# Gate matrices from one-hot rows: three bf16 pieces with four tokens innermost, in place of float32

## The chip, the core and the metric

The kernel runs on one NeuronCore of one Trainium2 chip. The metric is device time in microseconds (us). Five engines work side by side and meet at semaphores: TensorE (PE in the rows; PEld is its weight load), VectorE (DVE), ScalarE (ACT), GpSimd (POOL) and SyncE (SP), which issues most DMAs.

## The reference, cut to what matters

The layer is a token mixer followed by a product-key expert mixer (PEER). For every token and each of 8 heads, the mixer scores 128 × 128 experts as the sum of two key scores, keeps the best 16, and takes a softmax over them as gates:

```python
top_s, top_pos = lax.top_k(cand, PEER_TOPK)
idx = jnp.take_along_axis(cand_idx, top_pos, axis=-1)      # i1 * 128 + i2
gate = jax.nn.softmax(top_s, axis=-1)
act = jax.nn.gelu(jnp.einsum("td,thkd->thk", xb, expert_down[idx]))
return jnp.einsum("thk,thkd->td", gate * act, expert_up[idx])
```

There are 512 tokens, width 1024, and 128 picks (8 heads × 16) per token.

## The kernel before, in words

The first 128 tokens gather their experts' rows by indirect DMA. The other 384 (`TD`) do it densely: for all 128 × 128 experts the kernel computes GELU(x · down) on TensorE, multiplies by a gate matrix that is zero for experts that were not picked, and multiplies by `up` on TensorE.

The gate matrix of one token is 128 × 128, indexed by i2 and i1. It is made by a matrix product over the token's 128 picks, which lie on the partitions: one operand holds in row p the one-hot row of i2 times the gate of pick p, the other the one-hot row of i1. This stretch is called the gate stage here. It runs in 96 steps of four tokens (12 groups of 32 tokens, 8 steps each). In every step:

- the two operands `ob` and `oa` are made. In 67 of the 96 steps VectorE makes both: four TENSOR_SCALARs (line 850, one per token, compare with i2 and multiply by the gate) and one TENSOR_TENSOR over the four tokens (line 852, compare with i1). In the other 29 (`ng % 10 in A_ACT`) VectorE makes only the one-hot rows of i2 (line 841), and ScalarE makes the rows of i1 with the gate in them (lines 845 and 846);
- TensorE multiplies them into a PSUM bank `g_ps` (line 857, four float32 matmuls, which the trace shows as eight, two passes each), and ScalarE copies the bank to `stg` (line 860);
- `take` puts some products of another kind between: tiles of x · down (`s_ps`, lines 126 to 128) that are needed later. Their weights are split in a high and a low part, `w_hi` on ScalarE (line 612) and `w_lo` on GpSimd (line 613);
- in 28 of the steps a part of the top-16 search of the first 128 tokens is done on VectorE (`picks`: lines 671 to 721).

After every eighth step `stg` goes to DRAM by SyncE, and a small part to SBUF on GpSimd (line 866). The order on an engine comes from a scheduler that follows the code and its data; TensorE's is tied by `issue_after`. `ob` and `oa` have four buffers each. Behind the gate stage comes the longest stretch, in which TensorE multiplies by `up` (line 941) and makes the other tiles of x · down.

Of the kernel before, what the change touches and what calls it, by code (L numbers as in the profile page):

```python
# [18 lines left out]
P = 128  # L19
# [10 lines left out]
NK = 128  # L30
# [3 lines left out]
TD = NDT * P  # L34
# [38 lines left out]
def hymba_peer_block(ctx, tc, consts, x, nmix, w_in, w_ba, conv_w, a_log, dt_bias, dn_w, w_pool, pool_scale,  # L73
                     w_out, nffn, w_q, sub_k, downT, down, up, nfin, out):
    nc = tc.nc
# [8 lines left out]
    iota = cst[:, C_IO:C_IO + P]  # L84
# [64 lines left out]
    with ExitStack() as fx:  # L149
# [77 lines left out]
        with tc.tile_pool(name="prep", bufs=1) as pr:  # L227
# [59 lines left out]
            for h in range(DNH):  # L287
                for qk, dst in ((0, qT), (1, kT)):
# [3 lines left out]
                    for tb in range(NTB):  # L292
                        o = (tb * DNH + h) * 2 + qk
                        nc.tensor.matmul(ssq[:, o:o + 1], sq[:, tsl(tb)], ones[:, 0:1],
                                         start=(h == 0 and qk == 0 and tb == 0),
                                         stop=(h == 3 and qk == 1 and tb == 3))
            for h in range(DNH):
# [3 lines left out]
                for tb in range(NTB):  # L301
                    nc.tensor.transpose(pv[:, tsl(tb)], vt[:, tsl(tb)], ident)
                nc.vector.tensor_tensor(vb[:, :, h, :], v4(pv), beta[:, :, h:h + 1].broadcast_to([P, NTB, P]),
                                        op=ALU.mult)
# [9 lines left out]
                                           op0=ALU.mult, op1=ALU.mult)  # L314
# [3 lines left out]
            for tb in range(NTB):  # L318
# [3 lines left out]
                for h in range(DNH):  # L322
                    nc.tensor.matmul(gr[:, tsl(h)], gt[:, tb, h:h + 1].broadcast_to([P, P]), umat,
                                     start=(h == 0), stop=(h == 3))
                dt = pr.tile(H4, F32, name="dt")
                for h in range(DNH):
                    o = tb * 4 + h
                    nc.vector.scalar_tensor_tensor(dt[:, h], gr[:, tsl(h)], gcs[:, 0, o:o + 1], m0,
                                                   op0=ALU.subtract, op1=ALU.min)
# [5 lines left out]
                for lhs, dst in ((kT, d["at"]), (qT, d["aq"])):  # L335
# [3 lines left out]
                    for h in range(DNH):  # L339
                        nc.vector.scalar_tensor_tensor(dst[:, h], kk[:, tsl(h)], rqk[:, tb, h, 1:2], dt[:, h],  # L340
                                                       op0=ALU.mult, op1=ALU.mult)
                nc.vector.tensor_mul(qT[:, :, ts], qT[:, :, ts], egr)
                fr = p_dl.tile([P, 512], F32, name="fr", tag="dl")
                for h in range(DNH):
                    nc.tensor.matmul(fr[:, tsl(h)], fco[:, tb, h:h + 1].broadcast_to([P, P]), ident,
                                     start=(h == 0), stop=(h == 3))
# [26 lines left out]
        with ExitStack() as f2:  # L373
# [110 lines left out]
            for tb in range(NTB):  # L484
# [5 lines left out]
                for h in range(DNH):  # L490
                    nc.tensor.matmul(vps[:, tsl(h)], d["tt"][:, h], vb[:, tb, h], start=(h == 0),
                                     stop=(tb == 0 and h == 3))
# [24 lines left out]
                for h in range(DNH):  # L517
                    nc.tensor.matmul(ops[:, tsl(h)], d["aq"][:, h], vn[:, h], start=(tb == 0 and h == 0),
                                     stop=(h == 3))
# [65 lines left out]
    pp = ctx.enter_context(tc.tile_pool(name="pp", bufs=1))  # L585
# [3 lines left out]
    sc0 = pp.tile([P, NG, PH, 2, NK], F32, name="sc0")  # L589
    eidx = [pp.tile([P, NSLOT], I32, name=f"eidx{b}") for b in range(NG)]  # L590
    gat = [pp.tile([P, PH, K], F32, name=f"gat{b}") for b in range(NG)]
    i1t = pp.tile([P, TD], F32, name="i1t")
    n1t = pp.tile([P, TD], F32, name="n1t")
    i2t = pp.tile([P, TD], F32, name="i2t")
    gtt = pp.tile([P, TD], F32, name="gtt")
    ngt = pp.tile([P, TD], F32, name="ngt")

    gp = ctx.enter_context(tc.tile_pool(name="gp", bufs=2))
    up_p = ctx.enter_context(tc.tile_pool(name="up_p", bufs=2))
# [134 lines left out]
    with ExitStack() as fy:  # L734
        tk = fy.enter_context(tc.tile_pool(name="tk", bufs=2))
        p_pj = fy.enter_context(tc.tile_pool(name="p_pj2", bufs=2, space=PSUM))
        p_sc = fy.enter_context(tc.tile_pool(name="p_sc", bufs=4, space=PSUM))
        skt = tk.tile([P, 16, NK], F32, name="skt", bufs=1)
        nc.scalar.dma_start(out=skt, in_=sub_k)
        SA = [P, NDT, PH, K]  # L740
        i1a = tk.tile(SA, F32, name="i1a", bufs=1)
        i2a = tk.tile(SA, F32, name="i2a", bufs=1)
        tsa = tk.tile(SA, F32, name="tsa", bufs=1)

        def query(h, eng):
            qh = tk.tile([P, 2, T], F32, name="qh")
            w = [load_pair(w_q[2 * h + p], eng) for p in range(2)]
            ps = [p_pj.tile([P, 512], F32, name="q_ps") for p in range(2)]
            parts = [slice(0, T)] if h else [slice(0, T // 2), slice(T // 2, T)]
            for ts in parts:  # L750
                for p in range(2):
                    for c in range(DC):
                        mm3(ps[p][:, ts], (w[p][0][:, c, :], w[p][1][:, c, :]), (xn_hi[:, c, ts], xn_lo[:, c, ts]),
                            c == 0, c == DC - 1)
            for p in range(2):
                cp = nc.scalar.copy(qh[:, p], ps[p])
            behind[:] = [None, cp.ins]
            sc = tk.tile([P, NDT, 2, NK], F32, name="sc")
            ps = [p_sc.tile([P, 512], F32, name="sc_ps") for _ in range(NTB)]
            for p in range(2):  # L760
                for tb in range(NTB):
                    nc.tensor.matmul(ps[tb][:, p * NK:(p + 1) * NK], qh[:, p, tb * P:(tb + 1) * P],  # L762
                                     skt[:, 2 * h + p, :], start=(p == 0), stop=(p == 1))
            for tb in range(NTB):
                nc.scalar.copy(sc0[:, tb, h] if tb < NG else sc[:, tb - NG],
                               ps[tb][:, :2 * NK].rearrange("p (a k) -> p a k", a=2))
            return sc

        sc = query(0, nc.vector)
        for h in range(PH):  # L770
            sc_next = query(h + 1, nc.gpsimd) if h + 1 < PH else None
            for _ in topk(tk, sc, NDT, tsa[:, :, h, :], i1a[:, :, h, :], i2a[:, :, h, :]):
                pass
            sc = sc_next
            if sc is not None:
                make_ahead(h + 1)
        make_ahead(S_QUERY + S_WAIT)
        ex = tk.tile(SA, F32, name="ex", bufs=1)
        softmax(tk, ex.rearrange("p b h k -> p (b h) k"), tsa.rearrange("p b h k -> p (b h) k"), s_act[0])


        steps = ahead_steps()
        taken = 0
        pe_last = s_last[0]

        def take(goal):
            nonlocal taken, pe_last
            while taken < goal:
                with tc.issue_after(pe_last.ins):
                    next(steps, None)  # L790
                pe_last = s_last[0]
                taken += 1

        for src, dst in ((i1a, i1t), (i2a, i2t), (ex, gtt)):
            if src is ex:
                take(DC)
            ps = p_pj.tile([P, 512], F32, name="q_ps")
            with tc.issue_after(pe_last.ins):
                for b in range(NDT):
                    pe_last = nc.tensor.transpose(ps[:, b * P:(b + 1) * P], src[:, b].rearrange("p h k -> p (h k)"),  # L800
                                                  ident)
            nc.vector.tensor_copy(dst, ps[:, :TD])
            if dst is not i2t:
                nc.scalar.activation(n1t if dst is i1t else ngt, ps[:, :TD], AF.Copy, scale=-1.0)

    hp.append(ctx.enter_context(tc.tile_pool(name="hp2", bufs=RUN + 1 - RA)))

    with ExitStack() as fy:
# [17 lines left out]
        gs = fy.enter_context(tc.tile_pool(name="gs", bufs=3))  # L826
# [5 lines left out]
        for tg in range(NTG):  # L832
            stg = gs.tile([P, NK, TG], F32, name="stg", bufs=1)
            for q in range(TG // 4):
                oa = gs.tile([P, 4, P], F32, name="oa", bufs=4)
                ob = gs.tile([P, 4, P], F32, name="ob", bufs=4)
                ps = p_g.tile([P, 512], F32, name="g_ps")
                t0 = tg * TG + q * 4
                q4 = [P, 4, P]
                if ng % 10 in A_ACT:  # L840
                    one = nc.vector.tensor_tensor(ob, iota[:, None, :].broadcast_to(q4),  # L841
                                            i2t[:, t0:t0 + 4, None].broadcast_to(q4), op=ALU.is_equal)
                    for u in range(4):
                        t = t0 + u
                        nc.scalar.activation(oa[:, u], iota, AF.Abs, bias=n1t[:, t:t + 1])
                        nc.scalar.activation(oa[:, u], oa[:, u], AF.Relu, scale=ngt[:, t:t + 1], bias=gtt[:, t:t + 1])
                else:
                    for u in range(4):
                        t = t0 + u
                        nc.vector.tensor_scalar(ob[:, u], iota, i2t[:, t:t + 1], gtt[:, t:t + 1], op0=ALU.is_equal,  # L850
                                                op1=ALU.mult)
                    one = nc.vector.tensor_tensor(oa, iota[:, None, :].broadcast_to(q4),  # L852
                                            i1t[:, t0:t0 + 4, None].broadcast_to(q4), op=ALU.is_equal)
                ng += 1
                with tc.issue_after(pe_last.ins):
                    for u in range(4):
                        pe_last = nc.tensor.matmul(ps[:, u * P:(u + 1) * P], ob[:, u], oa[:, u], start=(u == 0),
                                                   stop=(u == 3))
                take(S_FIRST + ng * (n_steps - S_FIRST) // (TD // 4))
                nc.scalar.copy(stg[:, :, q * 4:q * 4 + 4], ps.rearrange("p (t i) -> p i t", i=NK))  # L860
                if ng * n_picks // (TD // 4) > picked:
                    with tc.issue_after(one.ins):
                        next(picks)
                    picked += 1
            sv = stg.rearrange("p i t -> p (i t)")
            nc.gpsimd.tensor_copy(gsb0[:, tg, :], sv[:, :GN * TG])
            nc.sync.dma_start(out=gmat[tg, :, GN * TG:], in_=sv[:, GN * TG:])
# [180 lines left out]
```

## Time and profile before

| | us |
|---|---|
| median of 3 runs | 1597.91 (1595.98 to 1601.22) |
| the profiled execution | 1597.25 |
| its span, first to last instruction | 1595.5 |
| TensorE busy | 1543.3 (97%) |
| TensorE weight loads busy | 1391.5 (87%) |
| VectorE busy | 1291.3 (81%) |
| ScalarE busy | 692.1 (43%) |
| GpSimd busy | 556.9 (35%) |

Busy time is that in which an engine had an instruction in work. Matmuls are pipelined and their ends are modelled, so a busy TensorE need not be at its limit: start-to-start times tell more. The shares are means over stages with different limits, so the gate stage has to be read by itself.

### The profile page before, as it was taken

How to read it: one execution, taken by the hardware profiler on the slowest of the kernel's cores; microseconds unless marked ns; L12 is line 12 of the kernel's file. 1: busy time of each engine (PE TensorE's matmuls, PEld its weight loads, DVE VectorE, ACT ScalarE, POOL GpSimd, SP SyncE). 2: the span in 40 equal slices, each digit the busy share in tenths (PEclk: the TensorE clock that was granted, in tenths of full speed). 3: DMA queues.
4: the chain of work that ended last, by engine and by line, in shares of the span. 5: the costliest groups of instructions: out<-in, count | busy, mean ns of one | idle time of the engine just before them, and what ended most of it. 6: DMA issues, size and time to landing. Idle time of an engine off the chain costs nothing.

```text
span 1595.5 us, 23368 instructions
## 1 busy us (share of the span) xinstructions
PE 1543.3 (97%) x8417; PEld 1391.5 (87%) x8417; DVE 1291.3 (81%) x2652; ACT 692.1 (43%) x1175; POOL 556.9 (35%) x362
## 2 busy tenths in 40 slices
PE   6999999999999899899999999999999999999996
PEld 5889798888899899889888888889989888888885
DVE  5577666699999999996887777778888787888885
ACT  5545343333338687673333333333333333333333
POOL 1000000144464333224454445444444444444331
PEclk9999999999999999999999999999999999999998
DMA  6221221422344455459999999999999999899971
GB/s 210 80 67 55 65 83 41 172 89 85 93 128 149 175 194 220 153 207 387 364 337 327 339 315 317 329 329 334 311 332 311 335 319 334 309 326 340 321 265 61
DMA packets 142388, 367.32 MB, mean 230 GB/s; under 512 B 11232, under 2 KB 65520, under 8 KB 140608
## 3 DMA queue, kind: packets, MB, share of 16 engines
q1 hardware_dynamic: 104416, 228.09, 41.4%
q0 software_dynamic: 37712, 136.69, 23.9%
q8 instruction: 66, 1.08, 0.3%
q10 hardware_dynamic: 144, 1.05, 0.2%
q14 instruction: 50, 0.41, 0.1%
HBM read 331.58 MB, written 34.21 MB: 229 GB/s over the span
## 4 chain that ended last, share of the span: by engine, by line
PE 80%; DVE 17%; ACT 1%; DMA 1%; issue 1%; POOL 1%; SPq 0%; ACTq 0%; DVEq 0%; POOLq 0%
PE acc L941 33%; PE s_ps L126 9%; PE s_ps L128 9%; PE s_ps L127 9%; DVE ob L850 7%; PE pj L127 3%; PE pj L126 3%; PE pj L128 3%; DVE oa L852 3%; PE q_ps L127 2%; PE q_ps L128 2%; PE q_ps L126 2%; PE ups L432 1%; PE p L441 1%; DVE ob L841 1%; PE sc_ps L762 1%
## 5 line engine op out<-in xcount | busy, mean ns | idle before, releaser
L126 PE MATMUL s_ps<-xn_hi,w_hi 128*128 128x384 f32 x1024 | 356.8, 348 | 0.0
L128 PE MATMUL s_ps<-xn_hi,w_lo 128*128 128x384 f32 x1024 | 346.4, 338 | 2.5 <-DVE w_lo L613 1.9
L127 PE MATMUL s_ps<-xn_lo,w_hi 128*128 128x384 f32 x1024 | 345.7, 338 | 0.0
L612 ACT ACTIVATE w_hi<-w_raw 128x1024 fp32r<-128x1024 f32 x144 | 152.9, 1062 | 331.7 <-PE s_ps L127 260.4
L916 POOL DMA_INDIRECT row<-in_down_dram,eidx x128 | 190.0, 1485 | 224.8 <-DVE row L918 194.4
L925 POOL DMA_INDIRECT row<-in_up_dram,eidx x128 | 187.0, 1461 | 222.8 <-DVE xr L927 201.0
L613 POOL TENSOR_TENSOR w_lo<-w_raw,w_hi 128x1024 fp32r<-128x1024 f32 x60 | 153.8, 2564 | 291.1 <-ACT w_hi L612 257.2
L941 PE MATMUL acc<-u_hi,whi 128*128 128x512 f32 x768 | 238.6, 391 | 0.6 <-ACT whi L120 0.6
L941 PE MATMUL acc<-u_lo,whi 128*128 128x512 f32 x768 | 237.6, 389 | 0.0
L941 PE MATMUL acc<-u_hi,wlo 128*128 128x512 f32 x768 | 237.5, 389 | 0.0
L120 ACT ACTIVATE whi<-w 128x384 fp32r<-128x384 f32 x128 | 67.2, 525 | 307.5 <-issue 277.2
L128 PEld LDWEIGHTS s_ps<-xn_hi,w_lo 128*128 128x128 f32 x1024 | 192.9, 188 | 3.5 <-DVE w_lo L613 2.3
L127 PEld LDWEIGHTS s_ps<-xn_lo,w_hi 128*128 128x128 f32 x1024 | 193.2, 189 | 3.2
L126 PEld LDWEIGHTS s_ps<-xn_hi,w_hi 128*128 128x128 f32 x1024 | 193.2, 189 | 3.2
L121 DVE TENSOR_TENSOR wlo<-w,whi 128x384 fp32r<-128x384 f32 x128 | 71.2, 556 | 133.8 <-ACT whi L120 133.6
L927 DVE SCALAR_TENSOR_TENSOR xr<-row,dots,xr 128x1024 f32<-128x1024 f32 x128 | 164.2, 1282 | 9.6 <-DMA row<-in_up_dram,eidx 7.7
L941 PEld LDWEIGHTS acc<-u_lo,whi 128*128 128x128 f32 x768 | 144.3, 188 | 31.3 <-DVE u_lo L121 0.3
L941 PEld LDWEIGHTS acc<-u_hi,wlo 128*128 128x128 f32 x768 | 144.2, 188 | 29.9
L918 DVE SCALAR_TENSOR_TENSOR row<-row,xg 128x1024 f32<-128x1024 f32 x128 | 152.1, 1220 | 15.0 <-DMA row<-in_down_dram,eidx 11.4
L941 PEld LDWEIGHTS acc<-u_hi,whi 128*128 128x128 f32 x768 | 143.0, 188 | 24.4 <-ACT whi L120 0.8
L121 DVE TENSOR_TENSOR u_lo<-u_raw,u_hi 128x1024 fp32r<-128x1024 f32 x128 | 156.0, 1219 | 4.1 <-ACT u_hi L120 4.1
L120 ACT ACTIVATE u_hi<-u_raw 128x1024 fp32r<-128x1024 f32 x128 | 134.3, 1049 | 5.5 <-DMA u_raw<-in_up_dram 2.8
(298 smaller groups left out, 2448.8 us busy)
## 6 DMA issues: line engine op xcount, KB each, us to landing
u_raw<-in_up_dram SPq DMA_DIRECT2D x128, 512.0 KB, 6.2
w_raw<-in_downT_dram SPq DMA_DIRECT2D x128, 512.0 KB, 5.7
gmat<-stg SPq DMA_DIRECT2D x12, 1984.0 KB, 8.4
gsb<-gmat SPq DMA_DIRECT2D x31, 768.0 KB, 7.3
w_raw<-in_w_in_dram SPq DMA_DIRECT2D x20, 512.0 KB, 3.6
w_raw<-in_w_q_dram SPq DMA_DIRECT2D x16, 512.0 KB, 3.6
hfar<-h_far SPq DMA_DIRECT2D x26, 192.0 KB, 2.0
h_act<-hfar SPq DMA_DIRECT2D x26, 192.0 KB, 5.9
```

Of the source, the lines that this page charges most:

```text
L120: nc.scalar.activation(hi, src, AF.Copy)
L121: nc.vector.tensor_sub(lo, src, hi.bitcast(F32))
L126: nc.tensor.matmul(ps, ahi, bhi, start=first, stop=False)
L127: nc.tensor.matmul(ps, ahi, blo, start=False, stop=False)
L128: return nc.tensor.matmul(ps, alo, bhi, start=False, stop=last)
L612: nc.scalar.activation(hi, raw, AF.Copy)
L613: eng.tensor_sub(lo, raw, hi.bitcast(F32))
L916: nc.gpsimd.indirect_dma_start(out=r, out_offset=None, in_=down, in_offset=bass.IndirectOffsetOnAxis(ap=eidx[b][:, s:s + 1], axis=0))
L918: nc.vector.scalar_tensor_tensor(r, r, 1.0, xg, op0=ALU.mult, op1=ALU.mult, accum_out=dots[:, s:s + 1])
L925: nc.gpsimd.indirect_dma_start(out=r, out_offset=None, in_=up, in_offset=bass.IndirectOffsetOnAxis(ap=eidx[b][:, s:s + 1], axis=0))
L927: nc.vector.scalar_tensor_tensor(xr[b], r, dots[:, s:s + 1], xr[b], op0=ALU.mult, op1=ALU.add)
L941: nc.tensor.matmul(acc[b][n], l[:, bs], r[:, n * 512:(n + 1) * 512], start=(i == 0 and l is whi and r is uhi), stop=(i == NK - 1 and l is ...
```

## The change

The gate is no longer a factor in float32. Ahead of the stage it is split into three bf16 pieces whose sum is the float32 gate (`gpc`), by three casts and two subtractions on VectorE. The one-hot rows and the pieces are bf16, and the tiles have the four tokens of a step innermost. Each step now makes the one-hot rows of i2 (`oh2`), multiplies them by the three pieces in one TENSOR_TENSOR (`ob`, 3 × 128 × 4 elements), and makes the rows of i1 (`oa`); in the 29 steps with ScalarE's help ScalarE makes only `oa`, now without the gate. TensorE adds three bf16 products per token.

```diff
-    i1t = pp.tile([P, TD], F32, name="i1t")
+    i1t = pp.tile([P, TD], BF16, name="i1t")
     n1t = pp.tile([P, TD], F32, name="n1t")
-    i2t = pp.tile([P, TD], F32, name="i2t")
+    i2t = pp.tile([P, TD], BF16, name="i2t")
     gtt = pp.tile([P, TD], F32, name="gtt")
-    ngt = pp.tile([P, TD], F32, name="ngt")
+    gpc = pp.tile([P, 3, TD], BF16, name="gpc")
+    iota4 = pp.tile([P, NK, 4], BF16, name="iota4")
+    nc.vector.tensor_copy(iota4, iota[:, :, None].broadcast_to([P, NK, 4]))
...
+        for j in range(3):
+            nc.vector.tensor_copy(gpc[:, j], gtt)
+            if j < 2:
+                nc.vector.tensor_sub(gtt, gtt, gpc[:, j])
...
-                oa = gs.tile([P, 4, P], F32, name="oa", bufs=4)
-                ob = gs.tile([P, 4, P], F32, name="ob", bufs=4)
+                oa = gs.tile([P, NK, 4], BF16, name="oa", bufs=4)
+                oh2 = gs.tile([P, NK, 4], BF16, name="oh2", bufs=2)
+                ob = gs.tile([P, 3, NK, 4], BF16, name="ob", bufs=4)
...
+                nc.vector.tensor_tensor(oh2, iota4, i2t[:, None, t4].broadcast_to(q4), op=ALU.is_equal)
+                one = nc.vector.tensor_tensor(ob, oh2[:, None].broadcast_to(p4), gpc[:, :, None, t4].broadcast_to(p4),
+                                              op=ALU.mult)
                 if ng % 10 in A_ACT:
-                    one = nc.vector.tensor_tensor(ob, iota[:, None, :].broadcast_to(q4),
-                                            i2t[:, t0:t0 + 4, None].broadcast_to(q4), op=ALU.is_equal)
                     for u in range(4):
-                        t = t0 + u
-                        nc.scalar.activation(oa[:, u], iota, AF.Abs, bias=n1t[:, t:t + 1])
-                        nc.scalar.activation(oa[:, u], oa[:, u], AF.Relu, scale=ngt[:, t:t + 1], bias=gtt[:, t:t + 1])
+                        ab = gs.tile([P, P], F32, name="ab", bufs=2)
+                        nc.scalar.activation(ab, iota, AF.Abs, bias=n1t[:, t0 + u:t0 + u + 1])
+                        nc.scalar.activation(oa[:, :, u], ab, AF.Relu, scale=-1.0, bias=1.0)
                 else:
-                    for u in range(4):
-                        t = t0 + u
-                        nc.vector.tensor_scalar(ob[:, u], iota, i2t[:, t:t + 1], gtt[:, t:t + 1], op0=ALU.is_equal,
-                                                op1=ALU.mult)
-                    one = nc.vector.tensor_tensor(oa, iota[:, None, :].broadcast_to(q4),
-                                            i1t[:, t0:t0 + 4, None].broadcast_to(q4), op=ALU.is_equal)
+                    one = nc.vector.tensor_tensor(oa, iota4, i1t[:, None, t4].broadcast_to(q4), op=ALU.is_equal)
                 ng += 1
                 with tc.issue_after(pe_last.ins):
                     for u in range(4):
-                        pe_last = nc.tensor.matmul(ps[:, u * P:(u + 1) * P], ob[:, u], oa[:, u], start=(u == 0),
-                                                   stop=(u == 3))
+                        for j in range(3):
+                            pe_last = nc.tensor.matmul(ps[:, u * P:(u + 1) * P], ob[:, j, :, u], oa[:, :, u],
+                                                       start=(u == 0 and j == 0), stop=(u == 3 and j == 2))
```

VectorE's order near the start of the gate stage, before. The rows L671 to L676 are the top-16 search; `ob` and `oa` are the operands of a step.

```order
L841 TENSOR_TENSOR ob<-cst,i2t 128x512
L850 TENSOR_SCALAR ob<-cst,i2t,gtt 128x128 x4
L852 TENSOR_TENSOR oa<-cst,i1t 128x512
L850 TENSOR_SCALAR ob<-cst,i2t,gtt 128x128 x4
L852 TENSOR_TENSOR oa<-cst,i1t 128x512
L671 MAX val<-sc_2702 128x8
L672 MAX_INDEX idx<-val,sc_2702 128x8
L674 MATCH_REPLACE rep<-val,sc_2702 128x128
```

The same place in VectorE's order of the changed kernel (the search's lines are L673 to L678 there, `oh_…` are the buffers of `oh2`):

```order
L673 MAX val<-sc_2702 128x8
L850 TENSOR_TENSOR oh_5007<-iota_2710,i2t 128x512
L674 MAX_INDEX idx<-val,sc_2702 128x8
L676 MATCH_REPLACE rep<-val,sc_2702 128x128
L851 TENSOR_TENSOR ob<-oh_5007,gpc 128x1536
L677 MAX val<-rep 128x8
L850 TENSOR_TENSOR oh_5047<-iota_2710,i2t 128x512
L678 MAX_INDEX idx<-val,rep 128x8
L851 TENSOR_TENSOR ob<-oh_5047,gpc 128x1536
L859 TENSOR_TENSOR oa<-iota_2710,i1t 128x512
L850 TENSOR_TENSOR oh_5073<-iota_2710,i2t 128x512
L859 TENSOR_TENSOR oa<-iota_2710,i1t 128x512
```

Every gate instruction is now a TENSOR_TENSOR with two operands in SBUF, and the scheduler puts some other instruction between an `oh2` and the `ob` that reads it: in all 96 steps the two are not neighbours. The search's instructions stand more thinly among them.

TensorE's order around one step of the gate stage, before:

```order
L127 MATMUL s_ps<-xn_lo,w_hi 128x384
L128 MATMUL s_ps<-xn_hi,w_lo 128x384
L857 MATMUL g_ps<-oa,ob 128x128 x4
L126 MATMUL s_ps<-xn_hi,w_hi 128x384
L127 MATMUL s_ps<-xn_lo,w_hi 128x384
```

And in the changed kernel (the first and the last of the twelve gate products):

```order
L128 MATMUL s_ps<-xn_hi,w_lo 128x384
L864 LDWEIGHTS ob
L864 MATMUL g_ps<-oa,ob 128x128
L864 LDWEIGHTS ob
L864 MATMUL g_ps<-oa,ob 128x128
...
L864 LDWEIGHTS ob
L864 MATMUL g_ps<-oa,ob 128x128
L126 MATMUL s_ps<-xn_hi,w_hi 128x384
```

The gate products stand at the same place among the tiles of x · down, twelve pairs of weight load and matmul in place of four float32 matmuls. GpSimd's order is the same in both.

## Rows read from the trace of the kernel before

**Rows 1.** Page, part 1: busy us, share of span, instructions.
```profile
PE 1543.3 (97%) x8417; PEld 1391.5 (87%) x8417; DVE 1291.3 (81%) x2652; ACT 692.1 (43%) x1175; POOL 556.9 (35%) x362
```

**Rows 2.** Windows: the gate stage, and what follows it.
```profile
core 0: us, PE busy (x) PEld busy (x) DVE busy (x) ACT busy (x) POOL busy (x), PEclk, DMA share, GB/s
482.60:711.30 228.70, 211.24 (x1442) 206.19 (x1441) 226.42 (x622) 170.70 (x388) 75.69 (x39) 0.99 0.51 184
711.30:1595.50 884.20, 869.23 (x4270) 777.40 (x4270) 700.11 (x900) 315.14 (x440) 387.31 (x264) 0.99 0.89 315
```

**Rows 3.** Chain of waits inside the gate stage, shares by line (cut by the view).
```profile
by line: DVE ob L850 47.8%; DVE oa L852 17.6%; DVE ob L841 7.6%; DVE rep L674 2.7%; DVE idx L672 2.5%; DVE idx L676 2.2%; DVE oh L714 2.1%; DVE i L721 2.1%; DVE oh L717 2.1%; DVE val L675 1.7%; DVE val L671 1.5%; DVE idf L686 1.3%; DVE ta L
```

**Rows 4.** Groups of instructions in the gate stage: count | busy us, mean ns.
```profile
L850 DVE TENSOR_SCALAR ob<-cst,i2t,gtt 128x128 f32<-128x128 f32 x268 | 117.4, 489 | 0.0
...
L126 PE MATMUL s_ps<-xn_hi,w_hi 128*128 128x384 f32 x225 | 84.7, 377 | 0.0
...
L841 DVE TENSOR_TENSOR ob<-cst,i2t 128x512 f32<-128x512 f32 x29 | 19.7, 679 | 0.0
```

**Rows 5.** Single lines: count, duration ns min/median/max, first and last start.
```profile
L850 DVE TENSOR_SCALAR ob<-cst,i2t,gtt x268: 320/336/2433, 483.7 to 705.0; 128x128 f32<-128x128 f32 x134
L852 DVE TENSOR_TENSOR oa<-cst,i1t x67: 662/679/691, 483.1 to 705.3; 128x512 f32<-128x512 f32 x67
L717 DVE TENSOR_TENSOR oh<-oh,idf x4: 685/690/2870, 543.3 to 708.6; 128x1024 bf16<-128x1024 bf16 x4
L717 DVE TENSOR_TENSOR oh<-oh,idf x8: 959/1996/3205, 331.5 to 470.8; 128x1536 bf16<-128x1536 bf16 x8
L714 DVE TENSOR_TENSOR oh<-fij,cst x8: 1757/1758/1761, 329.8 to 469.0; 128x1536 bf16<-128x1536 f32 x8
L704 DVE TENSOR_SCALAR ta<-pos x4: 167/172/2391, 540.1 to 705.9; 128x32 uint32<-128x32 uint32 x4
L686 DVE CAST idf<-idx x4: 184/313/2399, 523.8 to 690.9; 128x64 bf16<-128x64 uint32 x4
L613 POOL TENSOR_TENSOR w_lo<-w_raw,w_hi x27: 2362/2481/3127, 483.1 to 696.5; 128x1024 fp32r<-128x1024 f32 x27
```

**Rows 6.** VectorE in order of time, gate stage: start us, duration us.
```profile
494.90 3.18 DVE L850 TENSOR_SCALAR ob<-cst,i2t,gtt 128x128 f32<-128x128 f32 x4
498.01 0.68 DVE L852 TENSOR_TENSOR oa<-cst,i1t 128x512 f32<-128x512 f32 x1
498.61 1.10 DVE L850 TENSOR_SCALAR ob<-cst,i2t,gtt 128x128 f32<-128x128 f32 x4
499.63 0.68 DVE L852 TENSOR_TENSOR oa<-cst,i1t 128x512 f32<-128x512 f32 x1
```

**Rows 7.** GpSimd (first row) and VectorE in order of time around 602 us.
```profile
602.16 3.13 POOL L613 TENSOR_TENSOR w_lo<-w_raw,w_hi 128x1024 fp32r<-128x1024 f32 x1 [2.56 <-ACT w_hi L612]
...
601.77 0.68 DVE L852 TENSOR_TENSOR oa<-cst,i1t 128x512 f32<-128x512 f32 x1
602.37 0.68 DVE L841 TENSOR_TENSOR ob<-cst,i2t 128x512 f32<-128x512 f32 x1
602.97 0.29 DVE L671 MAX8 val<-sc 128x8 f32<-128x128 f32 x1
...
603.83 1.55 DVE L850 TENSOR_SCALAR ob<-cst,i2t,gtt 128x128 f32<-128x128 f32 x1
```

**Rows 8.** TensorE in order of time, one gate step and its neighbours.
```profile
563.38 1.05 PE L857 MATMUL g_ps<-oa,ob 128*128 128x128 f32 x8
564.19 0.42 PE L126 MATMUL s_ps<-xn_hi,w_hi 128*128 128x384 f32 x1
564.45 0.34 PE L127 MATMUL s_ps<-xn_lo,w_hi 128*128 128x384 f32 x1
...
565.33 1.05 PE L857 MATMUL g_ps<-oa,ob 128*128 128x128 f32 x8
```

More of the change, by code (lines that the diff above doesn't have):

```diff
@@ L802, in hymba_peer_block @@
             nc.vector.tensor_copy(dst, ps[:, :TD])
-            if dst is not i2t:
-                nc.scalar.activation(n1t if dst is i1t else ngt, ps[:, :TD], AF.Copy, scale=-1.0)
+            if dst is i1t:
+                nc.scalar.activation(n1t, ps[:, :TD], AF.Copy, scale=-1.0)
+        for j in range(3):
+            nc.vector.tensor_copy(gpc[:, j], gtt)
+            if j < 2:
+                nc.vector.tensor_sub(gtt, gtt, gpc[:, j])
     hp.append(ctx.enter_context(tc.tile_pool(name="hp2", bufs=RUN + 1 - RA)))
@@ L834, in hymba_peer_block @@
             for q in range(TG // 4):
-                oa = gs.tile([P, 4, P], F32, name="oa", bufs=4)
-                ob = gs.tile([P, 4, P], F32, name="ob", bufs=4)
+                oa = gs.tile([P, NK, 4], BF16, name="oa", bufs=4)
+                oh2 = gs.tile([P, NK, 4], BF16, name="oh2", bufs=2)
+                ob = gs.tile([P, 3, NK, 4], BF16, name="ob", bufs=4)
                 ps = p_g.tile([P, 512], F32, name="g_ps")
                 t0 = tg * TG + q * 4
-                q4 = [P, 4, P]
+                t4 = slice(t0, t0 + 4)
+                q4 = [P, NK, 4]
+                p4 = [P, 3, NK, 4]
+                nc.vector.tensor_tensor(oh2, iota4, i2t[:, None, t4].broadcast_to(q4), op=ALU.is_equal)
+                one = nc.vector.tensor_tensor(ob, oh2[:, None].broadcast_to(p4), gpc[:, :, None, t4].broadcast_to(p4),
+                                              op=ALU.mult)
                 if ng % 10 in A_ACT:
-                    one = nc.vector.tensor_tensor(ob, iota[:, None, :].broadcast_to(q4),
-                                            i2t[:, t0:t0 + 4, None].broadcast_to(q4), op=ALU.is_equal)
                     for u in range(4):
-                        t = t0 + u
-                        nc.scalar.activation(oa[:, u], iota, AF.Abs, bias=n1t[:, t:t + 1])
-                        nc.scalar.activation(oa[:, u], oa[:, u], AF.Relu, scale=ngt[:, t:t + 1], bias=gtt[:, t:t + 1])
-                else:
-                    for u in range(4):
-                        t = t0 + u
-                        nc.vector.tensor_scalar(ob[:, u], iota, i2t[:, t:t + 1], gtt[:, t:t + 1], op0=ALU.is_equal,
-                                                op1=ALU.mult)
-                    one = nc.vector.tensor_tensor(oa, iota[:, None, :].broadcast_to(q4),
-                                            i1t[:, t0:t0 + 4, None].broadcast_to(q4), op=ALU.is_equal)
+                        ab = gs.tile([P, P], F32, name="ab", bufs=2)
+                        nc.scalar.activation(ab, iota, AF.Abs, bias=n1t[:, t0 + u:t0 + u + 1])
+                        nc.scalar.activation(oa[:, :, u], ab, AF.Relu, scale=-1.0, bias=1.0)
+                else:
+                    one = nc.vector.tensor_tensor(oa, iota4, i1t[:, None, t4].broadcast_to(q4), op=ALU.is_equal)
                 ng += 1
```

## The prediction

> **What bounds the kernel now.** I read the page first. TensorE is busy 97% of the span and VectorE 81% [rows 1], which suggests a kernel bound by TensorE all through. The change, however, touches one stretch only, so the windows come next: from 482.6 to 711.3 us, 228.7 us, VectorE is busy 226.4 us and TensorE 211.2 us; behind it, for 884 us, TensorE is busy 869 us and VectorE 700 us [rows 2]. The reader is to see that the engine which is nearly full changes at these borders. The chain of waits in the stretch decides which of the two it is: its shares are VectorE's, line by line; L850, L852 and L841, the three instructions that make one-hot rows, have 73% between them, and the rest is the search [rows 3]. So the gate stage is as long as VectorE's queue. A saving on TensorE buys nothing there, and an instruction added on VectorE is paid in full.
>
> What is in VectorE's 228.7 us? The order of time gives the cost from start to start: the four TENSOR_SCALARs of a step 1.02 us (498.61 to 499.63), the TENSOR_TENSOR 0.60 us (498.01 to 498.61) [rows 6]. The same four took 3.11 us at 494.90. Those 2.09 us more are a hold. GpSimd's subtraction `w_lo` (27 in the stage, 2.36 us at least) and VectorE keep each other out: the longest TENSOR_SCALAR took 2433 ns where the median is 336 [rows 5]. The holds add up to 268 × (489 − 336) ns = 41.0 us on L850 [rows 4, 5], and one each of 2.2, 2.2 and 2.1 us on L717, L704 and L686 (maximum less median) [rows 5]: 47.5 us, 1.76 us per `w_lo`.
>
> **The change part by part.**
>
> *A bf16 TENSOR_TENSOR.* The stage has one already: L717 multiplies bf16 by bf16, one operand a short row that is read again and again, as here. Unheld it takes 685 ns for 1024 elements and 959 for 1536, so 274 ns per 512; on float32 input L714 takes 1758 ns for 1536 [rows 5]. So it runs at twice the rate, with some 137 ns fixed. 512 elements then take 411 ns. Successive instructions overlap by 0.08 us (679 ns long, 600 from start to start) [rows 5, 6], so `oh2` or `oa` costs 0.33 us of queue and `ob` (1536) 0.88 us.
>
> *Steps in which VectorE makes both operands, 67.* Before 1.02 + 0.60 = 1.62 us, now 0.33 + 0.88 + 0.33 = 1.54: 67 × (−0.08) = −5.4 us.
>
> *Steps in which ScalarE makes `oa`, 29* [rows 4]. Before, VectorE had one instruction of 0.60 us, because the gate went into ScalarE's half. Now the gate is on VectorE's side in every step: 0.33 + 0.88 = 1.21. That is 29 × 0.61 = +17.7 us, the largest term. It lies on VectorE's queue, which nothing covers. ScalarE, busy 170.7 of 228.7 us [rows 2], had room, and its small saving is worth nothing.
>
> *The split of the gate.* Two subtractions of 384 columns, at most 0.60 × 384/512 = 0.45 us each, and three casts, between the cast row L686 (0.2 to 0.3 us for 64 columns) and 0.45: +1.9 us on the same queue, ahead of the first `ob`. The copy that makes `iota4` stands before the search, is no dearer than the 0.60 us of L852, and gets 0 here and 0.6 at the upper end.
>
> *The holds.* An `oh2` has to be done before its `ob` starts, but the order always has another instruction between the two, so I add no gap there. What changes is how GpSimd meets VectorE. At 602.16 a `w_lo` came while one TENSOR_TENSOR ran, and a second followed directly; `w_lo` took 3.13 us, 0.77 more than its least, so it was let in only as the second one ended. Then four search instructions ran beside it, and the next TENSOR_SCALAR took 1.55 us, a hold of 1.21 [rows 7]. That the search's instructions run beside `w_lo` is why the mean hold is 1.76 and not 2.09. In the new order gate instructions stand between the search's, so after one or two of them a gate instruction is in front and waits. Bounds: at the top 27 × 2.09 = 56 us, +9; at the bottom no hold at all, −47.5. I take 2.0 us each, 54 us, +6.5, because the row that is like the new instructions (L717, two bf16 operands in SBUF) was held for 2.2 us.
>
> [...]
>
> *TensorE.* From one gate block to the next is 1.95 us with six `s_ps` passes at 0.176 us (564.45 to 565.33 is five starts), so a block costs 1.95 − 1.06 = 0.89 us, eight passes of 0.112 [rows 8]. 96 × 0.89 + 674 × 0.176 = 85 + 119 = 204 us of 228.7 (674 is about three lines of 225 [rows 4]). No bf16 product of 128 columns is in the trace. From below it costs a third of a 384-column pass, 0.059 us; from above what a float32 pass of 128 columns costs, 0.112. Twelve make 0.70 to 1.34 us, 96 times that 68 to 129, and the stage's TensorE work 187 to 248 us. I take the middle, 0.085, since the columns speak for the first and a weight load for every product for the second: 217 us. VectorE's new stage is longer than even the upper end, so TensorE adds 0 to the sum; this cover is thin there, and the first rival prices it.
>
> [...]
>
> *Elsewhere* nothing is added or removed. The 884 us behind the stage start when VectorE's queue and the last gate matrices are done, so they shift with it.
>
> *Sum.* The profiled execution took 1597.25 us (1.75 more than its span), 0.7 less than the median of the runs. −5.4 + 17.7 + 1.9 + 6.5 = +20.7: 1618 us. The forecast's own range goes from holds that stay as they are, with the casts at their least (1610), to holds at their top with 0.6 us for `iota4` and a few us of TensorE's lag (1626).
>
> **The rivals.**
>
> *TensorE becomes the bound.* It decides from 0.113 us per product, where 1152 × 0.113 + 119 = 249 us is VectorE's new length. In favour: twelve weight loads per step, where a load takes part in a price of 0.112 now; and a TensorE that waits more may be granted less than the 0.99 of full clock [rows 2]; against: half the bytes per element. At 0.13 the stage is 269 us, +40, 1637.
>
> *The doubled rate does not come.* The repeated row of L717 is 16 bf16 long, here it is four. At the float32 rates (0.60 and 1758 − 80 = 1.68 us) a step costs 2.88 instead of 1.62 and 2.28 instead of 0.60: 84 + 49 = +133, with the split and the holds 1739 us. [...]
>
> *Faster: the holds end.* One mechanism: TENSOR_SCALARs waited for `w_lo`, TENSOR_TENSORs of the gate don't, as the 67 of L852 never did [rows 5]. Then 41.0 us of L850 go, and the rest of the sum, +14.2, stays: 1597.25 + 14.2 − 41.0 = 1570 us. It comes out faster as soon as more than 14.2 us of holds go in all, that is, below 1.2 us per `w_lo`. A partial form is likelier than the full one: GpSimd, kept waiting by back-to-back TENSOR_TENSORs, gets in beside the search and holds little.
>
> *No change.* The holds fall by some 14 us and just pay for the rest: 1597.
>
> **How the numbers follow.** Forecast 0.60 (1618). TensorE as the bound 0.14. Single rate 0.05. Faster 0.11. No change 0.10. Under 0.3%, some 5 us, a difference cannot be told from none here. Slower is 0.60 + 0.14 + 0.05 = 0.79, same 0.10, faster 0.11. The range reaches down to 1596, which leaves out the faster cases and a little of no change (about 0.13), and up to 1645, which takes in TensorE at 0.13 and leaves out the single rate (with the worst of TensorE, 0.07).
>
> **What would show it.** In the changed profile the gate stage should be about 249 us, with VectorE busy nearly all of it and named in the chain; `oh2` and `oa` about 0.41 us, `ob` about 0.96 us, and a few of either near 2.4 us or above; the sum of these excesses near 54 us; `w_lo` longer than before, because it is kept waiting. TensorE should wait for `ob` or `oa` and have 217 us of work. I am wrong if `ob` takes 1.7 us, if the excesses are below 30 us, or if VectorE shows waits for TensorE in the stage. The stretch behind it should again be 884 us.

## The result: 25.9 us slower, and TensorE bounds the changed stage

The changed kernel takes 1623.25 us (median of four runs, 1622.13 to 1624.02), the kernel before 1597.35 us beside it (four runs): the ratio of the runs is 1.0154, with a 95% interval from 1.0141 to 1.0167 (the two medians alone give 1.0162). The forecast was 1618 us, slower, with VectorE as the bound. The time lies in the forecast's range and the sign is right; the bound is not.

The page after, part 1 (busy us, share of the span, instructions) and the engines' shares of part 4, the chain that ended last.

```profile
PE 1586.9 (98%) x8801; PEld 1423.0 (88%) x8801; DVE 1303.5 (80%) x2553; ACT 682.5 (42%) x1174; POOL 565.0 (35%) x362
...
PE 93%; DVE 3%; issue 1%; ACT 1%; DMA 1%; POOL 1%; SPq 0%; ACTq 0%; DVEq 0%; POOLq 0%
```

The windows of the gate stage and of what follows it, for the changed kernel; the columns are those of [rows 2].

```profile
482.60:737.80 255.20, 252.03 (x1797) 234.83 (x1797) 237.51 (x521) 159.08 (x382) 81.42 (x38) 0.99 0.46 164
737.80:1622.20 884.40, 871.25 (x4284) 779.30 (x4282) 698.70 (x898) 314.37 (x440) 386.93 (x265) 0.99 0.89 315
```

The stage has grown from 228.7 to 255.2 us, by 26.5; the stretch behind it is again 884 us [rows 2]. So all of the loss lies in the stage. There the engine that is nearly full has changed: TensorE is busy 252.0 of 255.2 us (before 211.2 of 228.7), VectorE 237.5 (before 226.4 of 228.7).

The chain of waits inside the changed stage, shares by line:

```profile
by line: PE g_ps L864 51.1%; PE s_ps L126 14.1%; PE s_ps L127 14.0%; PE s_ps L128 13.8%; issue 6.0%; POOL w_lo L615 1.0%; ACT w_hi L614 0.4%
```

VectorE's one-hot lines, which had 73% of it before [rows 3], are gone from the chain. It runs from one product on TensorE to the next, half of it in the gate's own line 864. (`issue` is time for which the profile shows no wait.) The waits say the same from the other side (who waited <- for whom: us in all, times, longest):

```profile
DVE ob L851 <- PE g_ps L864: 11.6, 23, 1.4
PE g_ps L864 <- DVE ob L851: 3.2, 1, 3.2
DVE oa L859 <- PE g_ps L864: 2.4, 4, 0.9
```

VectorE waits 14.0 us for a gate product to give its operand buffer back; TensorE waits for `ob` once, 3.2 us, at the first gate product. Before the change no operand of the gate on VectorE waited for TensorE.

The price of a gate block, in TensorE's order of time (start us, duration us); it answers to [rows 8]:

```profile
565.87 1.59 PE L864 MATMUL g_ps<-oa,ob 128*128 128x128 bf16 x12
567.22 0.42 PE L126 MATMUL s_ps<-xn_hi,w_hi 128*128 128x384 f32 x1
567.48 0.34 PE L127 MATMUL s_ps<-xn_lo,w_hi 128*128 128x384 f32 x1
568.36 1.59 PE L864 MATMUL g_ps<-oa,ob 128*128 128x128 bf16 x12
```

From block to block are 2.49 us with six `s_ps` passes of 0.176 us, which leaves 1.43 us for a block, against 0.89 before. The twelve products lie 0.118 us apart: the block lasts 1.59 us, one product 0.297 (row below), and (1.59 − 0.297) / 11 = 0.118. Between the first and the last of the 96 blocks stand 628 passes, so TensorE has 96 × 1.43 + 628 × 0.176 = 137 + 111 = 248 us of work there. From 489.1 to 737.8 us, where it does this work, are 248.7 us, and the profile shows it busy in all of them.

Single lines of the changed kernel (count, duration ns min/median/max, first and last start), the answer to [rows 5]:

```profile
L850 DVE TENSOR_TENSOR oh<-iota,i2t x96: 396/410/2502, 480.1 to 726.2; 128x512 bf16<-128x512 bf16 x96
...
L851 DVE TENSOR_TENSOR ob<-oh,gpc x96: 928/946/3146, 485.9 to 727.7; 128x1536 bf16<-128x1536 bf16 x96
...
L859 DVE TENSOR_TENSOR oa<-iota,i1t x67: 397/411/2096, 482.9 to 728.6; 128x512 bf16<-128x512 bf16 x67
...
L864 PEld LDWEIGHTS <-ob x1152: 111/117/148, 489.1 to 737.7; 128*128 128x128 bf16 x192
L864 PE MATMUL g_ps<-oa,ob x1152: 278/297/330, 489.1 to 737.8; 128*128 128x128 bf16 x192
...
L615 POOL TENSOR_TENSOR w_lo<-w_raw,w_hi x27: 2387/2530/6537, 480.1 to 722.3; 128x1024 fp32r<-128x1024 f32 x27
```

`oh2` and `oa` take 0.41 us and `ob` 0.95, as forecast (0.41 and 0.96). A few are held, up to 3.1 us.

### The profile page after: what moved, and what is told of

It is laid out like the page before. It is cut to its first block, busy times and chain, and to the rows that moved or that the text cites. A ratio compares the mean times of both kernels' runs of the same rounds, so it can differ in the third digit from the quotient of the medians.

```text
span 1622.2 us, 24027 instructions
## 1 busy us (share of the span) xinstructions
PE 1586.9 (98%) x8801; PEld 1423.0 (88%) x8801; DVE 1303.5 (80%) x2553; ACT 682.5 (42%) x1174; POOL 565.0 (35%) x362
## 4 chain that ended last, share of the span: by engine, by line
PE 93%; DVE 3%; issue 1%; ACT 1%; DMA 1%; POOL 1%; SPq 0%; ACTq 0%; DVEq 0%; POOLq 0%
PE acc L948 32%; PE s_ps L126 11%; PE s_ps L127 11%; PE s_ps L128 11%; PE g_ps L864 8%; PE pj L127 3%; PE pj L126 3%; PE pj L128 3%; PE q_ps L127 2%; PE q_ps L128 2%; PE q_ps L126 2%; PE ups L432 1%; PE p L441 1%; PE sc_ps L764 1%; POOL w_lo L615 1%
## 5 line engine op out<-in xcount | busy, mean ns | idle before, releaser
L615 POOL TENSOR_TENSOR w_lo<-w_raw,w_hi 128x1024 fp32r<-128x1024 f32 x60 | 158.9, 2649 | 299.8 <-ACT w_hi L614 276.7
L948 PE MATMUL acc<-u_lo,whi 128*128 128x512 f32 x768 | 237.5, 389 | 0.0
L864 PE MATMUL g_ps<-oa,ob 128*128 128x128 bf16 x1152 | 152.1, 297 | 3.2 <-DVE ob L851 3.2
```

The costliest lines, as they stand in the source:

```text
L615: eng.tensor_sub(lo, raw, hi.bitcast(F32))
L864: pe_last = nc.tensor.matmul(ps[:, u * P:(u + 1) * P], ob[:, j, :, u], oa[:, :, u], start=(u == 0 and j == 0), stop=(u == 3 and j == 2))
L948: nc.tensor.matmul(acc[b][n], l[:, bs], r[:, n * 512:(n + 1) * 512], start=(i == 0 and l is whi and r is uhi), stop=(i == NK - 1 and l is ...
```

## The experiments

The theory after the result (A): a gate product costs 0.118 us because `oa`, which TensorE reads as the moving operand, has the four tokens innermost, so that it is read at a step of four bf16 (8 bytes); with this price TensorE bounds the stage. Rivals: (B) the weights, read from `ob` at the same step, or the weight load itself, set the price; (C) VectorE's new queue is the bound all the same, and TensorE is only its follower. The expectations of the runs have letters of their own: for one piece, for two pieces and for the changed kernel with `w_lo` moved, their theory A is only that TensorE bounds the stage, and their theory B is (C) here. Chains of waits in this section are those from 489 to 690 us.

**VectorE alone.** Only the first piece's product is made; VectorE's work is untouched.

```diff
-                        for j in range(3):
+                        for j in range(1):
...
```

> The changed kernel with only the first of the three bf16 pieces multiplied on TensorE (four products in a step, not twelve); VectorE still makes all three pieces of every step, in the same order. Left out: the second and third piece of the gate in the product. Theory A (TensorE bounds the changed gate stage: 96 blocks of 1.42 us and 674 passes of 0.176 us make its 255 us): TensorE's work falls by 96 x 8 x 0.119 = 91 us to some 164 us, and the stage falls to what VectorE's queue needs, 222 to 236 us: 1589 to 1603 us. Theory B (as forecast, VectorE's queue bounds it and TensorE only looks full): the stage and the time stay, 1620 to 1626 us.

Measured: 1603.76 us (1602.57 to 1611.33 in seven runs), ratio 1.0044 [1.0029, 1.006]. The window of its stage and the chain by line:

```profile
482.60:716.00 233.40, 186.70 (x1036) 161.01 (x1035) 233.19 (x518) 155.28 (x381) 96.78 (x38) 0.89 0.50 182
```

```profile
by line: DVE ob L851 32.2%; DVE oh L850 16.1%; DVE oa L859 10.2%; issue 9.3%; PE g_ps L864 4.7%; PE s_ps L126 3.8%; PE s_ps L127 3.5%; PE s_ps L128 3.3%; DVE rep L676 2.5%; DVE val L673 1.5%; ACT stg L867 1.4%; DVE idf L688 1.3%; DVE fij L7
```

VectorE is busy in 233.2 of 233.4 us and leads the chain, as (A) says of a TensorE with a third of the products. The time came out 0.8 us above the range expected. So VectorE's queue by itself makes the kernel slower, but here by 5.5 us (by its interval between 4.6 and 9.6), not by 20.7; the next pair of runs gives it 12.5. TensorE is granted 0.89 of its clock here where it waits, against 0.99 in the changed kernel, and it does not matter, since VectorE sets the pace.

**Which operand.** First the weights read densely, then the moving operand; both leave everything else as it is, but the gate values are then those of other rows and tokens.

```diff
-  matmul(ps[...], ob[:, j, :, u], oa[:, :, u], ...)
+  matmul(ps[...], ob[:, j, u*32:(u+1)*32].rearrange("p a b -> p (a b)"), oa[:, :, u], ...)   # weights dense
+  matmul(ps[...], ob[:, j, :, u], oa[:, u*32:(u+1)*32].rearrange("p a b -> p (a b)"), ...)   # moving operand dense
```

> The changed kernel, where each product reads its 128 weights as neighbours in ob and not at a stride of four elements; the moving operand and all of VectorE's work stay. The elements are then those of other rows and tokens, so the gate values are not the right ones. If the stride of the weights makes a product cost 0.119 us: it falls to 0.06 to 0.09, TensorE's work to 188 to 222 us, VectorE bounds the stage, 1589 to 1605 us. If a bf16 weight load costs that at any stride: no change, 1620 to 1626 us.

> The changed kernel, where each product reads its moving operand as 128 neighbours in oa and not at a stride of four elements; the weights keep their stride. The gate values are not the right ones. If the stride of the moving operand makes the price: 1589 to 1605 us. If the weight load does: no change, 1620 to 1626 us.

Measured: weights dense 1621.44 us, 1.0145 [1.0128, 1.0162], as expected for weights that do not set the price; moving operand dense 1610.76 us, 1.0076 [1.006, 1.0093]. That lies between the two ranges expected: the price fell as it should, but VectorE needs more than the 222 to 236 us of stage that the lower range was built on (from 482.6 to 720.5 us, where the last gate product starts, VectorE is busy 237.0 of 237.9 us). One gate block on TensorE with dense weights, and its line:

```profile
567.16 1.55 PE L864 MATMUL g_ps<-oa,ob 128*128 128x128 bf16 x12
568.46 0.43 PE L126 MATMUL s_ps<-xn_hi,w_hi 128*128 128x384 f32 x1
...
L864 PE MATMUL g_ps<-oa,ob x1152: 274/294/330, 489.4 to 734.8; 128*128 128x128 bf16 x192
```

And with a dense moving operand, with the first operation behind it:

```profile
566.75 0.86 PE L864 MATMUL g_ps<-oa,ob 128*128 128x128 bf16 x12
567.42 0.42 PE L126 MATMUL s_ps<-xn_hi,w_hi 128*128 128x384 f32 x1
```

And the line's loads and products in that kernel:

```profile
L864 PEld LDWEIGHTS <-ob x1152: 110/113/152, 489.3 to 720.4; 128*128 128x128 bf16 x192
L864 PE MATMUL g_ps<-oa,ob x1152: 216/219/330, 489.3 to 720.5; 128*128 128x128 bf16 x192
```

The block shrinks from 1.59 to 0.86 us by the moving operand alone: (0.86 − 0.219) / 11 = 0.058 us per product. Dense weights leave it at 1.55. In the fast block the weights are still read at 8 bytes and a load still lasts 113 ns (117 in the changed kernel), and yet products start twice as often; neither was the limit. (B) falls. VectorE then bounds the stage (from its first to its last gate instruction it has 0.8 us of gaps in 238.0): the loss falls from 25.9 us to 12.5, and no further.

**How wide a step.** The moving operand read at two bf16 (4 bytes) instead of four, with the other work as it is:

```diff
-  oa[:, :, u]
+  oa[:, (u//2)*64:(u//2)*64+64].rearrange("p a b -> p (a b)").rearrange("p (i v) -> p i v", v=2)[:, :, u % 2]
```

> The changed kernel, where each product reads its moving operand at a stride of two bf16 elements (4 bytes) and not four (8 bytes); the gate values are not the right ones. In the changed kernel a product starts 0.118 us after the last, with the moving operand as neighbours 0.056. If any stride doubles the price: 0.118 again, 1620 to 1626 us. If the price goes by how many bytes a product runs through: 0.056 to 0.09, the stage falls to VectorE's own length, 1602 to 1612 us.

Measured: 1609.99 us, 1.0074 [1.0057, 1.009], in the lower range expected. One block of it:

```profile
567.59 0.90 PE L864 MATMUL g_ps<-oa,ob 128*128 128x128 bf16 x12
568.30 0.42 PE L126 MATMUL s_ps<-xn_hi,w_hi 128*128 128x384 f32 x1
```

With 0.221 us for one product it is (0.90 − 0.221) / 11 = 0.062 us. A step of 4 bytes is nearly free here (0.062 against 0.058 us dense), one of 8 bytes doubles the price (0.118).

**Two pieces in place of three.** `gpc` and `ob` lose the third piece, TensorE a third of its products.

```diff
-        for j in range(3):
+        for j in range(2):
...
-                ob = gs.tile([P, 3, NK, 4], BF16, name="ob", bufs=4)
+                ob = gs.tile([P, 2, NK, 4], BF16, name="ob", bufs=4)
...
```

> The changed kernel with the gate in two bf16 pieces and not three (left out: what is below the 16th bit of a gate), on VectorE (ob of 1024 elements) and on TensorE (eight products). Theory A: TensorE 96 x 8 x 0.119 + 119 = 210 us; VectorE's queue falls by 96 x 0.27 = 26 us from the 222 to 236 it needs now; the stage is 205 to 215 us, 1575 to 1588 us, faster than both. Theory B: only VectorE's 26 us go, 1594 to 1600 us.

Measured: 1586.23 us, 0.9924 [0.9908, 0.9941], in the range of their theory A. Here VectorE and TensorE are nearly even. TensorE's window (to 700 us) is 209.8 busy of 217.4 us, VectorE's 216.2; the window's row:

```profile
482.60:700.00 217.40, 209.81 (x1430) 191.70 (x1429) 216.23 (x518) 156.99 (x385) 81.15 (x38) 1.00 0.53 191
```

A third of the products less takes 96 × 4 × 0.118 = 45 us from TensorE, and `ob` with 1024 elements makes VectorE's queue shorter too: the loss of 25.9 us turns into a gain of 12.1, and both engines are then nearly full.

**The holds taken away, in three kernels.** `w_lo` of the gate stage goes from GpSimd to VectorE, so that no `w_lo` on GpSimd is left to hold it, at the price of 27 subtractions more on its queue. On a stage that VectorE bounds this should gain, on one that TensorE bounds it should not: the test between (A) and (C).

```diff
-                    pair = load_pair(downT[ahead[made[0]]], nc.gpsimd)
+                    pair = load_pair(downT[ahead[made[0]]], nc.vector)
...
```

> The kernel before with one edit: w_lo of the gate stage on VectorE and not on GpSimd. Theory A (VectorE's queue with 48 us of holds bounds the stage before): 223 - 48 + 31 = 206 us, about what TensorE needs (204): 1578 to 1588 us. If the holds cost nothing: VectorE has 31 us more, 1620 to 1630 us. If TensorE bounded the stage before, too: no change, 1595 to 1600 us.

> The changed kernel with the same edit: w_lo of the gate stage on VectorE. Theory A (TensorE bounds the changed stage with 250 us): VectorE falls to some 219 us and nothing is gained: 1617 to 1626 us. Theory B (VectorE bounds it): 18 us less, 1602 to 1609 us.

> Two gate pieces, as in the experiment before (left out: what is below the 16th bit of a gate), and the subtractions w_lo of the gate stage on VectorE and not on GpSimd, so that nothing on GpSimd reads SBUF beside the gate instructions but twelve small copies. If the holds are time lost by VectorE: 213 - 55 of holds + 27 x 1.14 = 189 us on VectorE, and TensorE's 204 us become the bound: 1574 to 1581 us. If the holds are only another place where VectorE waits anyway, the 31 us of subtractions add: 1605 to 1618 us.

Measured: the kernel before goes from 1598.42 to 1575.34 us (0.9851 [0.9834, 0.9869]), better than expected; the changed kernel to 1629.74 (1.0196 [1.0179, 1.0213], where it was 1.0154 without the edit), some 4 us worse than expected; the one with two pieces to 1584.36 (0.9913 [0.9897, 0.993]). That is short of what was expected, and its interval overlaps that of two pieces alone, 1.9 us above it. In the chains of the three kernels no `ob` is held any more: four TENSOR_SCALARs of the kernel before take 1.03 us at most (unheld 1.02, held 3.11 [rows 6]), an `ob` of the changed kernel 0.87, and one of the kernel with two pieces 0.64. The changed kernel with this edit, chain by line:

```profile
by line: PE g_ps L864 47.9%; PE s_ps L127 12.8%; PE s_ps L126 12.7%; PE s_ps L128 12.2%; DVE w_lo L615 3.0%; ACT w_hi L614 2.9%; ACT oa L857 1.5%; DVE i L723 1.2%; issue 0.9%; ACT stg L867 0.9%; DVE ob L851 0.9%; DVE oa L859 0.8%; ACT ab L8
```

Its window:

```profile
482.60:740.00 257.40, 251.79 (x1796) 233.28 (x1796) 214.26 (x540) 157.80 (x379) 12.35 (x11) 1.00 0.45 162
```

And two of its waits:

```profile
DVE w_lo L615 <- ACT w_hi L614: 40.9, 24, 4.1
ACT w_hi L614 <- PE s_ps L127: 36.5, 13, 6.1
```

VectorE has 43 us of idle time in its 257.4 us, TensorE 5.6. It stands 40.9 us behind `w_hi`, and ScalarE's `w_hi` waits 36.5 us for the products on TensorE that still read the buffer (the second row). The edit that is worth 23 us where VectorE bounds gains nothing here and costs some 6 us: (C) falls. With two pieces the chain shows that TensorE became the bound as soon as the holds were gone, which is why the edit gave nothing that can be told from the noise:

```profile
by line: PE g_ps L864 37.3%; PE s_ps L126 14.7%; PE s_ps L127 14.7%; PE s_ps L128 14.3%; ACT w_hi L614 3.6%; DVE w_lo L615 3.0%; ACT oa L857 2.0%; issue 1.7%; DVE ob L851 1.5%; DVE i L723 1.2%; DVE oh L716 1.1%; DVE oa L859 1.0%; ACT h_far 
```

**Pairs of tokens.** `oa` is laid out as two pairs, so that TensorE reads it at 4 bytes and VectorE still works on runs of two; `ob` stays. ScalarE writes its rows of `oa` to the same layout (not shown).

```diff
-                oa = gs.tile([P, NK, 4], BF16, name="oa", bufs=4)
+                oa = gs.tile([P, 2, NK, 2], BF16, name="oa", bufs=4)
...
-                    one = nc.vector.tensor_tensor(oa, iota4, i1t[:, None, t4].broadcast_to(q4), op=ALU.is_equal)
+                    one = nc.vector.tensor_tensor(oa, iota2[:, None].broadcast_to(o4), i1t[:, t4].rearrange(
+                        "p (a v) -> p a v", v=2)[:, :, None].broadcast_to(o4), op=ALU.is_equal)
...
-                           ... oa[:, :, u], ...
+                           ... oa[:, u // 2, :, u % 2], ...
```

> The changed kernel with oa laid out in two pairs of tokens (the moving operand at a stride of 4 bytes), all three pieces and all values as in the changed kernel. If TensorE's price is the stride of the moving operand: 0.06 us a product, VectorE's queue bounds the stage with its holds (some 238 us): 1603 to 1612 us. If the run of two bf16 on VectorE breaks the doubled rate, oa costs 0.60 and not 0.33 us in 67 steps: 18 us more, 1622 to 1630 us.

> The same with w_lo of the gate stage on VectorE: all three pieces, cheap products, no holds. VectorE 140 + 2 + 72 = 214 us, TensorE 96 x 0.75 + 114 = 186 us: VectorE bounds it, 1583 to 1593 us, faster than before, but slower than the kernel before with the same edit (1575), because three pieces cost VectorE more than TensorE saves. If TensorE's stall were the only thing wrong with the change, it would come out under 1575 us.

> The same with two gate pieces (left out: what is below the 16th bit of a gate). VectorE 114 + 1 + 72 = 187 us, TensorE 96 x 0.5 + 114 = 162 us: 1560 to 1570 us, the fastest of all. If something else (ScalarE, the DMA of the gate matrices) takes over at 200 us, as far as the kernel before came with the edit: 1574 to 1580 us.

Measured: pairs alone 1611.23 us (1.008 [1.0064, 1.0097]) and pairs with `w_lo` on VectorE 1584.49 (0.9911 [0.9894, 0.9927]), both as expected; the same with two pieces 1555.16 (0.9733 [0.9717, 0.975]), 5 us better than expected and the fastest of all. The pairs' `oa` on VectorE:

```profile
L862 DVE TENSOR_TENSOR oa<-iota,i1t x67: 396/410/2628, 483.8 to 718.2; 128x512 bf16<-128x512 bf16 x67
```

And its line of gate products, with one block on TensorE in the same kernel:

```profile
L868 PE MATMUL g_ps<-oa,ob x1152: 217/221/330, 490.0 to 722.0; 128*128 128x128 bf16 x192
...
566.82 0.90 PE L868 MATMUL g_ps<-oa,ob 128*128 128x128 bf16 x12
567.53 0.42 PE L126 MATMUL s_ps<-xn_hi,w_hi 128*128 128x384 f32 x1
```

`oa` costs VectorE what it cost before (0.41 us), and TensorE has the low price, (0.90 − 0.221) / 11 = 0.062. The kernel is then where the dense read had it, 13 us above the kernel before, with VectorE as the bound. With the holds gone too (its chain has two `ob` in at most 1.74 us) it gets to 1584; its window (to 700 us):

```profile
482.60:700.00 217.40, 200.48 (x1820) 181.39 (x1819) 214.96 (x545) 149.80 (x387) 24.37 (x11) 0.98 0.54 192
```

That is still 9 us above the kernel before with the same edit (1575). From its first to its last gate instruction VectorE takes 212.5 us here and 200.3 there, with gaps of 2.2 and 1.0 us: three exact pieces cost it more than float32 did. Of the kernels run here that keep all three pieces or the float32 gate, the old one with `w_lo` on VectorE is the fastest. Only two pieces, which leave out what is below a gate's 16th bit, turn this round. The window of that kernel's stage:

```profile
482.60:672.00 189.40, 176.53 (x1432) 157.73 (x1431) 188.13 (x540) 146.23 (x383) 24.87 (x12) 0.98 0.62 223
```

The stage is down to 189 us, with VectorE busy in nearly all of it and TensorE's 176.5 us close behind.

## Why the prediction was right in time and wrong in its bound

**The step that failed** is the term for TensorE: "I take the middle, 0.085", with 0.112 as the bound from above, and from it "TensorE adds 0 to the sum". It measured 0.118, over the upper bound. The bound was taken from a float32 pass, which reads its columns side by side; the new operand's layout was weighed for VectorE alone, though the diff shows `oa[:, :, u]` in the matmul. With 0.118 the prediction's own formula gives 1152 × 0.118 + 119 = 255 us of stage, and 255.2 came. To the last us that is chance: the 674 passes are those of the window before, and the changed window has 646, which makes 250 us; the rest is a wait of 3.2 us before the first gate product and some 2 us that the formula does not hold. That TensorE becomes the bound was the first rival, held at 0.14, with a point of decision (0.113) that the measured price passes; its reasons (a load per product, a lower clock) were not the ones that acted: the load is nearly the same in the fast block (113 ns against 117), and the granted clock stayed at 0.99.

**VectorE's gate instructions** were sized well. From its first to its last gate instruction VectorE's time in the traces can be sorted, start to start. The gate's instructions unheld take 126.3 us before and 138.4 with the dense moving operand, where VectorE is the bound: +12.1, forecast −5.4 + 17.7 = +12.3. The split of the gate takes 1.9 us unheld, as forecast.

**The holds** (what instructions took more than 0.1 us beyond the median of their line and operation, summed over that stretch) are 47.5 us before and 52.0 with the dense moving operand; the forecast was 54. In the changed kernel they are 48.5, beside 14 us of gaps in which VectorE waits anyway. Another measure of an instruction's normal time moves these terms, and those below, by some 2 us against each other; their total stays.

**What the sum left out.** Two things went the other way. The search's instructions take 45.7 us in place of 49.1, and VectorE's gate work starts 2.8 us earlier (480.3 instead of 483.1). The first may come from the search's new places between the gate's instructions; no run tried it alone. The second comes from what stands ahead of the stage: VectorE's copy of the gates, which precedes all gate work, itself starts at 479.63 us in the changed kernel and at 482.61 in the kernel before; why is open. So 12.1 + 1.9 + 4.5 − 3.4 − 2.8 = +12.3 us, and the kernel with the dense moving operand is 12.5 us slower than before. VectorE alone would have made some 1610 us, so the forecast was about 8 too high on this engine, and TensorE's 26 us took the place of the whole sum. The nearness of 1618 to 1623 is thus luck: the engine that set the time stood in the sum with 0, and the other's part was forecast too long. One thing stays open: with one piece VectorE's stretch is 231.7 us, with the dense moving operand 238.0, though its instructions are the same; 4.5 of the 6.3 us are the search's and 1.0 holds, and why these differ was not tried.

**The prediction's own tests.** `oh2`, `oa` and `ob` as forecast; the excesses above the 30 us named; `w_lo` longer (up to 6.54 us). "I am wrong if … VectorE shows waits for TensorE in the stage" is the test that caught it. The doubled rate on VectorE came (`ob` takes 0.95 us for 1536 elements, where float32 input took 1.76 [rows 5]), so the rival of 1739 is dead. The holds did not end by themselves, so the faster rival's mechanism did not act; that its lever was real the kernel before shows, where `w_lo` on VectorE gains 23 us.

## What to carry to other kernels

A layout that suits the engine which writes a tile has to be priced at the engine which reads it too: write down the step in bytes of every matmul's moving operand, and where no row shows that step, keep the bound open upwards. When two engines' loads in a stage lie within a few per cent, a forecast of the time can be right with the wrong bound; an edit that helps one engine alone (here `w_lo` moved off GpSimd) tells which it is. A change to one engine's queue is summed over the whole queue: what the others' instructions gain between the new ones belongs in it.

## What the runs showed of the hardware

The moving operand's step sets the price of a bf16 product with 128 columns: 0.058 us dense, 0.062 at 4 bytes, 0.118 at 8 bytes. From 566 to 569 us, where these blocks stand, the granted clock is 1.00 in the changed kernel, and the `s_ps` passes that follow the first one behind a block start 0.17 to 0.18 us apart on the mean in each of the traces. Steps of more than 8 bytes were not tried. The step of the weights does next to nothing: (1.55 − 0.294) / 11 = 0.114 us with dense weights against 0.118 at 8 bytes, and with a dense moving operand 0.058 although the weights stay at 8 bytes.

ScalarE feels the step of what it writes. Its `oa` at 8 bytes in the changed kernel:

```profile
L857 ACT ACTIVATE oa<-ab x116: 475/502/627, 482.4 to 726.6; 128x128 bf16<-128x128 f32 x116
```

And at 4 bytes in the kernel with pairs, 502 against 342 ns for 128 elements (with the dense moving operand, where only TensorE's read differs from the changed kernel, it is 508):

```profile
L860 ACT ACTIVATE oa<-ab x116: 328/342/435, 483.3 to 712.9; 128x128 bf16<-128x128 f32 x116
```

VectorE's doubled rate held at runs of two bf16 with a repeated row as the other operand (0.41 us for 512, row of L862 above; 0.68 for float32 [rows 5]).

GpSimd's `w_lo` took up to 6.54 us, where the shortest took 2.39. The longest `w_lo` of the changed kernel (first row) and VectorE around it, in order of time:

```profile
610.88 6.54 POOL L615 TENSOR_TENSOR w_lo<-w_raw,w_hi 128x1024 fp32r<-128x1024 f32 x1 [8.11 <-ACT w_hi L614]
...
610.79 0.94 DVE L851 TENSOR_TENSOR ob<-oh,gpc 128x1536 bf16<-128x1536 bf16 x1
611.65 0.42 DVE L859 TENSOR_TENSOR oa<-iota,i1t 128x512 bf16<-128x512 bf16 x1
611.99 0.42 DVE L850 TENSOR_TENSOR oh<-iota,i2t 128x512 bf16<-128x512 bf16 x1
612.33 0.41 DVE L859 TENSOR_TENSOR oa<-iota,i1t 128x512 bf16<-128x512 bf16 x1
612.66 0.95 DVE L851 TENSOR_TENSOR ob<-oh,gpc 128x1536 bf16<-128x1536 bf16 x1
613.53 0.75 DVE L850 TENSOR_TENSOR oh<-iota,i2t 128x512 bf16<-128x512 bf16 x2
614.20 0.95 DVE L851 TENSOR_TENSOR ob<-oh,gpc 128x1536 bf16<-128x1536 bf16 x1
615.07 0.28 DVE L673 MAX8 val<-sc 128x8 f32<-128x128 f32 x1
616.76 1.47 DVE L851 TENSOR_TENSOR ob<-oh,gpc 128x1536 bf16<-128x1536 bf16 x1 [1.41 <-PE g_ps L864]
```

`w_lo` came at 610.88 and ended at 617.42. If it needed no more than the shortest, an estimate, it began in effect at about 615.0, as the last of eight two-input instructions that follow each other without a gap was ending (615.15). The next one of VectorE's then took 1.47 us instead of 0.95.
